# A two-expert weighted sum: the last two tiles in one slot, and twelve product rows in place of ten on GpSimd

## The chip, the core and the metric

The kernel runs on one core of a Trainium2 chip. The core has engines that run side by side and wait for each other through semaphores: VectorE (DVE in the profile), ScalarE (ACT), GpSimd (POOL), TensorE (PE, not used here) and SyncE (SP, which here only issues transfers). Sixteen DMA engines move data between the chip's main memory (HBM) and the core's own memory (SBUF, 128 partitions). The metric is the device time of one execution in microseconds; the median over several runs is compared.

## The reference

For each of 16 x 1,024 = 16,384 tokens there are two expert outputs of 512 float32 values and two weights. The result is their weighted sum:

```
weights = combine_weights[..., np.newaxis]            # (16, 1024, 2, 1)
np.sum(expert_outputs * weights, axis=2)              # (16, 1024, 2, 512) -> (16, 1024, 512)
```

So 67.1 MB are read, 33.6 MB are written, and each output value takes two multiplications and one addition.

## The kernel before, in words

Each partition handles 128 tokens (`per`), in nine tiles (`sizes`): seven of 16 tokens, numbered 0 to 6, and two of 8, numbered 7 and 8. The first 120 tokens of every partition lie together in one region of the input, the last 8 in another (`rows`, line 37). A token is 4 KB in a partition: 1,024 float32, expert 0 and then expert 1. Seen as rows of 512 values, a tile of 16 tokens has 32 product rows.

A loop over the tiles (line 73) writes down for each:

- **A slot.** `et` (line 74) is taken from a pool of three slots, each large enough for 16 tokens. The tile that takes a slot for the fourth time and later has to wait until the store of the tile three places earlier has landed. So the load of tile 3 waits for the store of tile 0, and so on; the load of tile 7 waits for the store of tile 4, the load of tile 8 for the store of tile 5.
- **The load** (line 80), issued by SyncE. Tile 0 is loaded in two pieces.
- **The products**, tiles 0 to 6: GpSimd multiplies the last 10 of the 32 rows in place (line 117, `theirs`), VectorE the first 22 (line 122, `mine`). VectorE takes its weights from a copy in PSUM (`pw`), GpSimd from SBUF (`wt`). GpSimd's product is made to wait for the sum of the previous tile (line 121).
- **The sum** (line 123), on VectorE, of the two halves of each token. The result is packed into the front of the same slot (`ot`, line 76).
- **The store** (line 127), issued by ScalarE for tiles 0 to 6 and by SyncE for tiles 7 and 8.

Tile 7 is split in another way: ScalarE scales expert 0 of five tokens (line 114), GpSimd of three (line 117), and VectorE scales expert 1 (line 122) and adds (line 123). Tile 8 goes token by token: ScalarE scales expert 0 (line 88), and VectorE multiplies expert 1 and adds in one instruction (line 91). Both are the same before and after.

Each engine carries out its own instructions in the order written, and each queue issues its transfers in that order. Loads, and the two last stores, go through SyncE's queue, q1 in the profile; the other stores go through ScalarE's queue, q10. Both are served by the same sixteen DMA engines.

Of the kernel before, what the change touches and what calls it, by code (L numbers as in the profile page):

```python
# [1 line left out]

# [4 lines left out]


@with_exitstack
def kernel(  # L10
    ctx: ExitStack,
    tc: tile.TileContext,
    expert_outputs: bass.AP,
    combine_weights: bass.AP,
    out: bass.AP,
):

    nc = tc.nc
    b, s, k, h = expert_outputs.shape
    assert k == 2
    n = b * s
    P = nc.NUM_PARTITIONS
    per = n // P
    assert per * P == n
    sizes = [16] * 7 + [8, 8]
    J, LAST = max(sizes), sizes[-1]  # L30
    main = per - LAST
    assert sum(sizes) == per
    eo = expert_outputs.rearrange("b s k h -> (b s) (k h)")
    cw = combine_weights.rearrange("b s k -> (b s) k")
    o = out.rearrange("b s h -> (b s) h")

    def rows(x):

        a = x[0 : P * main, :].rearrange("(p t) f -> p t f", p=P)
        b = x[P * main : n, :].rearrange("(p t) f -> p t f", p=P)  # L40
        return lambda t, c: a[:, t : t + c, :] if t < main else b[:, t - main : t - main + c, :]

    eo, cw, o = rows(eo), rows(cw), rows(o)

    dt = mybir.dt.float32
    mult = mybir.AluOpType.mult
    add = mybir.AluOpType.add
    copy = mybir.ActivationFunctionType.Copy

    last = len(sizes) - 1  # L50

    wpool = ctx.enter_context(tc.tile_pool(name="w", bufs=1))
    ipool = ctx.enter_context(tc.tile_pool(name="in", bufs=3))
    ppool = ctx.enter_context(tc.tile_pool(name="pw", bufs=1, space=bass.MemoryType.PSUM))

    wt = wpool.tile([P, per * k], dt)

    for t, c in ((0, main), (main, LAST)):
        nc.scalar.dma_start(  # L59
            out=wt[:, k * t : k * (t + c)].rearrange("p (t k) -> p t k", k=k), in_=cw(t, c)  # L60
        )

    warm = wpool.tile([P, 1], dt)
    nc.scalar.activation(out=warm, in_=nc.const_aps.tensor(1.0, (P, 1), dt), func=copy)  # L64

    pw = ppool.tile([P, per * k], dt)
    nc.vector.tensor_copy(out=pw, in_=wt)  # L67
    w1 = pw.rearrange("p (t k) -> p t k", k=k)
    sync = mybir.DependencyInfo(mybir.DependencyClass.Sync, mybir.DependencyReason.DATA)
    total = None  # L70
    t0 = 0

    for g, c in enumerate(sizes):
        et = ipool.tile([P, J, k * h], dt)

        ot = et.rearrange("p j f -> p (j f)")[:, 0 : J * h].rearrange("p (j f) -> p j f", f=h)
        ek = et.rearrange("p j (k h) -> p (j k) h", k=k)

        for a, m in ((0, 2), (2, c - 2)) if g == 0 else ((0, c),):
            nc.sync.dma_start(  # L80
                out=et[:, a : a + m],
                in_=eo(t0 + a, m),
                max_dma_last_dim=k * h * 4 if g + a == 0 else None,
            )
        if g == last:
            for i in range(c):
                t = t0 + i
                nc.scalar.activation(  # L88
                    out=et[:, i, 0:h], in_=et[:, i, 0:h], func=copy, scale=wt[:, 2 * t : 2 * t + 1]
                )  # L90
                nc.vector.scalar_tensor_tensor(  # L91
                    out=ot[:, i, :],
                    in0=et[:, i, h : 2 * h],
                    scalar=wt[:, 2 * t + 1 : 2 * t + 2],
                    in1=et[:, i, 0:h],
                    op0=mult,
                    op1=add,
                )
        else:
            if g < last - 1:  # L100

                a, b = 2 * (c - 5), 2 * c
                mine, theirs = ek[:, 0:a], ek[:, a:b]
                wv = pw[:, 2 * t0 : 2 * t0 + a].unsqueeze(2)
                wp = wt[:, 2 * t0 + a : 2 * t0 + b].unsqueeze(2)
            else:

                m = c - 3
                mine, theirs = et[:, 0:c, h : 2 * h], et[:, m:c, 0:h]
                wv = w1[:, t0 : t0 + c, 1:2]  # L110
                wp = wt.rearrange("p (t k) -> p t k", k=k)[:, t0 + m : t0 + c, 0:1]
                for i in range(m):
                    t = t0 + i
                    nc.scalar.activation(  # L114
                        out=et[:, i, 0:h], in_=et[:, i, 0:h], func=copy, scale=wt[:, 2 * t : 2 * t + 1]
                    )
            p = nc.gpsimd.tensor_tensor(  # L117
                out=theirs, in0=theirs, in1=wp.to_broadcast(list(theirs.shape)), op=mult
            )
            if total is not None:  # L120
                tc.add_manual_dep(p.ins, total.ins.name, sync, reason="the shared port")
            nc.vector.tensor_tensor(out=mine, in0=mine, in1=wv.to_broadcast(list(mine.shape)), op=mult)  # L122
            total = nc.vector.tensor_tensor(  # L123
                out=ot[:, 0:c], in0=et[:, 0:c, 0:h], in1=et[:, 0:c, h : 2 * h], op=add
            )
        queue = nc.scalar if g < last - 1 else nc.sync
        queue.dma_start(out=o(t0, c), in_=ot[:, 0:c])
        t0 += c

# [1 line left out]
_INS = ['expert_outputs', 'combine_weights']  # L131
_OUTS = [((16, 1024, 512), 'float32')]


# [23 lines left out]
```

## Time and profile before

| | |
|---|---|
| median of 5 runs | 243.13 us (242.01 to 244.05) |
| profiled execution, its own time | 242.97 us |
| its span | 241.2 us |
| VectorE busy | 158.6 us |
| GpSimd busy | 64.0 us |
| ScalarE busy | 9.7 us |
| moved | 100.80 MB, 418 GB/s over the span |
| load of tile 7 issued / tile 8 issued | 183.00 us / 206.02 us |
| stores of tiles 6, 7, 8 issued | 214.66, 223.54, 229.23 us |

The profile is of one execution. All times inside it count from the start of its span; what lies around the span (1.8 us here) is in the execution's time and not in the trace. A group of instructions is shown with its total busy time, the mean duration of one in ns, and the idle time of its engine just before it with what ended that idle time. The row of DMA slices gives the mean busy share of the sixteen DMA engines in tenths.

### The profile page before, as it was taken

The numbers are of one execution on the slowest core, as the hardware profiler recorded it, in microseconds if no ns is written. First come the engines' busy times: TensorE is split into PE (matmuls) and PEld (weight loads), VectorE is DVE, ScalarE is ACT, GpSimd is POOL, SyncE is SP. The second block draws the span as 40 slices with busy tenths as digits, with TensorE's granted clock in tenths as the row PEclk, the third lists the DMA queues.
The fourth block names the chain that finished last, engine by engine and source line by source line (L and its number), as shares of the span: only waits on it lengthen the run. The fifth ranks groups of instructions, "written<-read, shape, count | busy, mean of one in ns | idle before, by whom it ended". The sixth has DMA issues, their size and how long they took to land.

```text
span 241.2 us, 165 instructions
## 1 busy us (share of the span) xinstructions
DVE 158.6 (66%) x25; ACT 9.7 (4%) x15; POOL 64.0 (27%) x12
## 2 busy tenths in 40 slices
DVE  0001999999749990059982999149990089999900
ACT  2000000000000000000000000000000000221600
POOL 0001920670049000058002920049000086030000
DMA  9998989989989989999989899989999899999994
GB/s 347 457 400 383 522 348 522 348 359 429 516 348 435 522 348 435 435 435 435 522 348 495 375 462 467 435 370 435 397 489 435 359 435 435 386 435 402 399 432 185
DMA packets 3152, 100.80 MB, mean 418 GB/s; under 512 B 464, under 2 KB 592, under 8 KB 848
## 3 DMA queue, kind: packets, MB, share of 16 engines
q1 hardware_dynamic: 1856, 71.30, 69.6%
q10 hardware_dynamic: 1296, 29.49, 28.5%
HBM read 67.24 MB, written 33.55 MB: 418 GB/s over the span
## 4 chain that ended last, share of the span: by engine, by line
DMA 55%; DVE 35%; another core or an unknown queue 2%; ACT 2%; issue 1%; ACTq 0%; DVEq 0%; SPq 0%
DMA out_dram<-et 24%; DMA et<-in_expert_outputs_dram 22%; DVE et L122 20%; DVE et L123 14%; DMA wt<-in_combine_weights_dram 9%; ACT et L88 2%; DVE et L91 1%; DVEq L153 0%; ACTq L153 0%; ACTq L59 0%; DVE pw L67 0%; DVEq L123 0%; SPq L80 0%; ACTq L88 0%
## 5 line engine op out<-in xcount | busy, mean ns | idle before, releaser
L122 DVE TENSOR_TENSOR et<-et,pw 128x11264 f32<-128x11264 f32 (+1 forms) x8 | 87.6, 10952 | 46.4 <-DMA et<-in_expert_outputs_dram 46.4
L117 POOL TENSOR_TENSOR et<-et,wt 128x5120 f32<-128x5120 f32 (+1 forms) x8 | 63.8, 7979 | 153.2 <-DMA et<-in_expert_outputs_dram 111.3
L123 DVE TENSOR_TENSOR et<-et 128x8192 f32<-128x8192 f32 (+1 forms) x8 | 65.3, 8158 | 0.9
L67 DVE COPY pw<-wt 128x256 f32<-128x256 f32 x1 | 0.4, 428 | 23.1 <-DMA wt<-in_combine_weights_dram 23.1
L114 ACT ACTIVATE et<-et,wt 128x512 f32<-128x512 f32 x5 | 3.2, 709 | 206.4 <-DMA et<-in_expert_outputs_dram 206.4
L91 DVE SCALAR_TENSOR_TENSOR et<-et,wt 128x512 f32<-128x512 f32 x8 | 5.6, 745 | 0.2
L88 ACT ACTIVATE et<-et,wt 128x512 f32<-128x512 f32 x8 | 5.0, 712 | 9.2 <-DMA et<-in_expert_outputs_dram 9.2
L64 ACT ACT_TABLE_LOAD x1 | 1.3, 1283 | 1.7 <-PEq L142 1.7
L64 ACT ACTIVATE warm<-const-float32-1.0 128x1 f32<-128x1 f32 x1 | 0.2, 203 | 0.0
L142 POOL MEMSET const-float32-0.0<- 128x1 f32 x1 | 0.1, 99 | 0.2 <-issue 0.2
L142 POOL MEMSET const-bfloat16-1.0<- 128x1 bf16 x1 | 0.1, 102 | 0.0
L142 POOL MEMSET const-uint8-127<- 128x1 uint8 x1 | 0.1, 102 | 0.0
L142 POOL MEMSET const-float32-1.0<- 128x1 f32 x1 | 0.1, 99 | 0.0
## 6 DMA issues: line engine op xcount, KB each, us to landing
out_dram<-et ACTq DMA_DIRECT2D x7, 4096.0 KB, 29.0
et<-in_expert_outputs_dram SPq DMA_DIRECT2D x2, 4096.0 KB, 21.3
et<-in_expert_outputs_dram SPq DMA_DIRECT2D x1, 7168.0 KB, 21.7
out_dram<-et SPq DMA_DIRECT2D x2, 2048.0 KB, 11.4
et<-in_expert_outputs_dram SPq DMA_DIRECT2D x1, 1024.0 KB, 5.2
wt<-in_combine_weights_dram ACTq DMA_DIRECT2D x1, 120.0 KB, 4.2
et<-in_expert_outputs_dram SPq DMA_DIRECT2D x6, 37.1
wt<-in_combine_weights_dram ACTq DMA_DIRECT2D x1, 8.0 KB, 21.8
```

The lines of the kernel that those rows point to most:

```text
L64: nc.scalar.activation(out=warm, in_=nc.const_aps.tensor(1.0, (P, 1), dt), func=copy)
L67: nc.vector.tensor_copy(out=pw, in_=wt)
L88: nc.scalar.activation(out=et[:, i, 0:h], in_=et[:, i, 0:h], func=copy, scale=wt[:, 2 * t : 2 * t + 1])
L91: nc.vector.scalar_tensor_tensor(out=ot[:, i, :], in0=et[:, i, h : 2 * h], scalar=wt[:, 2 * t + 1 : 2 * t + 2], in1=et[:, i, 0:h], op0=mul ...
L114: nc.scalar.activation(out=et[:, i, 0:h], in_=et[:, i, 0:h], func=copy, scale=wt[:, 2 * t : 2 * t + 1])
L117: p = nc.gpsimd.tensor_tensor(out=theirs, in0=theirs, in1=wp.to_broadcast(list(theirs.shape)), op=mult)
L122: nc.vector.tensor_tensor(out=mine, in0=mine, in1=wv.to_broadcast(list(mine.shape)), op=mult)
L123: total = nc.vector.tensor_tensor(out=ot[:, 0:c], in0=et[:, 0:c, 0:h], in1=et[:, 0:c, h : 2 * h], op=add)
L142: nc = _bacc.Bacc("TRN2", target_bir_lowering=False, num_devices=1)
```

## The change

Two things change.

1. Tile 8 no longer takes a slot of its own. Tiles 7 and 8, 8 tokens each, share one 16-token slot: tile 7 in its first half, tile 8 in its second. The only wait for that slot is the one at tile 7's load, for the store of tile 4; tile 8's load is next on SyncE's queue and has no wait of its own. The store of tile 5 is no longer waited for before the end.
2. In tiles 0 to 6 GpSimd multiplies 12 of the 32 product rows and VectorE 20. For GpSimd this is 6,144 elements in a partition where it was 5,120, for VectorE 10,240 where it was 11,264.

The number and the order of the instructions on each engine are the same.

```
-        et = ipool.tile([P, J, k * h], dt)
+        both = both[:, J - c : J] if g == last else ipool.tile([P, J, k * h], dt, name="et")
+        et = both[:, 0:c]

-        ot = et.rearrange("p j f -> p (j f)")[:, 0 : J * h].rearrange("p (j f) -> p j f", f=h)
+        ot = et.rearrange("p j f -> p (j f)")[:, 0 : c * h].rearrange("p (j f) -> p j f", f=h)
...
             if g < last - 1:

-                a, b = 2 * (c - 5), 2 * c
+                a, b = 2 * (c - 6), 2 * c
                 mine, theirs = ek[:, 0:a], ek[:, a:b]
```

## The prediction

> **What bounds the kernel now.** I read the page's slices first, because a kernel that moves 100.8 MB and computes little should be measured against its transfers.
>
> ```profile
> span 241.2 us, 165 instructions
> DVE 158.6 (66%) x25; ACT 9.7 (4%) x15; POOL 64.0 (27%) x12
> ...
> DMA  9998989989989989999989899989999899999994
> ...
> HBM read 67.24 MB, written 33.55 MB: 418 GB/s over the span
> ```
>
> The DMA row stands at 8 or 9 in every slice but the last. No compute engine is busy beyond 66%. Next I read stretches of the span (columns: stretch, its length, then busy us and instruction count of VectorE, ScalarE and GpSimd, granted clock, DMA share, GB/s).
>
> ```profile
> 0.00:4.00 4.00, 0.00 (x0) 1.49 (x2) 0.20 (x4) 1.00 0.52 162
> ...
> 84.00:124.00 40.00, 25.34 (x3) 0.00 (x0) 8.73 (x1) 1.00 0.97 419
> 124.00:160.00 36.00, 22.22 (x3) 0.00 (x0) 8.73 (x1) 1.00 1.00 432
> 160.00:183.00 23.00, 20.58 (x2) 0.00 (x0) 8.73 (x1) 1.00 1.00 417
> 183.00:206.00 23.00, 11.95 (x2) 0.00 (x0) 8.72 (x1) 1.00 0.99 426
> 206.00:222.00 16.00, 15.87 (x3) 3.17 (x5) 2.75 (x1) 1.00 1.03 416
> 222.00:232.00 10.00, 6.99 (x9) 5.01 (x8) 0.00 (x0) 1.00 0.95 410
> 232.00:237.40 5.40, 0.00 (x0) 0.00 (x0) 0.00 (x0) 1.00 0.98 422
> 237.40:241.20 3.80, 0.00 (x0) 0.00 (x0) 0.00 (x0) 1.00 0.15 65
> ```
>
> The last column but one is the answer: from 4 us to 237.4 us the 16 DMA engines have work in hand all the time (shares a little over 1 come from putting a packet into the stretch where it starts). They are empty only at the start, and thin in the last 3.8 us. The last packets explain that tail: eleven engines finish between 237.3 and 237.8, five between 239.3 and 239.8. The five fell behind around 163 to 171 us, where some 64 KB reads took 3.0 to 3.5 us and the usual one takes 2.42. At the best steady rate here, 434 GB/s, 100.8 MB take 232.3 us. The other 8.9 us of the span are start (2.6), slow packets and uneven engines, and the closing waits (1.4, from the last packet at 239.8 to 241.2).
>
> The groups by shape and the waits say the same from the compute side.
>
> ```profile
> L122 DVE TENSOR_TENSOR et<-et,pw 128x11264 f32<-128x11264 f32 x7 | 83.2, 11886 | 46.4 <-DMA et<-in_expert_outputs_dram 46.4
> L117 POOL TENSOR_TENSOR et<-et,wt 128x5120 f32<-128x5120 f32 x7 | 61.1, 8726 | 141.2 <-DMA et<-in_expert_outputs_dram 111.3 <-issue 17.4 <-DVE et L123 12.5
> L123 DVE TENSOR_TENSOR et<-et 128x8192 f32<-128x8192 f32 x7 | 60.8, 8692 | 0.7
> ...
> L122 DVE TENSOR_TENSOR et<-et,pw 128x4096 f32<-128x4096 f32 x1 | 4.4, 4414 | 0.0
> ...
> L117 POOL TENSOR_TENSOR et<-et,wt 128x1536 f32<-128x1536 f32 x1 | 2.8, 2750 | 12.0 <-DVE et L123 12.0
> ```
>
> VectorE waits 46.4 us for loads ahead of its product. The chain of waits alone misleads: it gives VectorE 35% of the span, because a load waits for a store and a store for a sum. But while one tile goes round that loop, other transfers fill the DMA engines. A shorter loop only helps if it fills an empty DMA slot, and there is none in the middle.
>
> **What the Trainium skill says.** "DMA: Bandwidth & Descriptors", section "Queues, rings and completion order": each DMA engine goes round the queues with work, a packet at a time, and takes one queue's descriptors in ring order. The trace agrees: between 203 and 205 us every engine alternates one 32 KB read and one 32 KB write, 1.21 us each, and tile 8's reads start only behind tile 7's. The same page, "Where 436 GB/s comes from", puts the ceiling at 435 GB/s; the steady 434 stands on it. "SBUF — State Buffer", "Who interferes with whom": VectorE with two SBUF inputs excludes a GpSimd operation that reads SBUF, with one it does not, and DMA contends with neither. The product reads its weights from PSUM, and indeed 11,264 elements take the same 11.89 us in all seven tiles with GpSimd beside them.
>
> **Part 1, the shared slot.** Before, tile 8's load waits for the store of tile 5, which lands at 205.94; the load is issued at 206.02. After, it stands behind tile 7's load (issued 183.00) with no wait of its own, so it is issued near 183.3, 22.7 us sooner. What it gains is only what the DMA engines were missing. They weren't: tile 7's own reads hold the queue until 207.2 on the fast engines and 209.2 on the late five, so tile 8's reads cannot start sooner than that. On the first eight or nine engines they arrive just in time: their first packets took 1.6 to 2.15 us and not 1.21, about 0.6 us each. Early issue may remove that, but these are engines that have 2 us to spare at the end. Value 0, ends -0.6 and 0. Nothing new queues behind the load on SyncE: the next there is the store of tile 7 at 223.5. Tile 8's data and products stay as they are; VectorE and ScalarE drop a wait that was over long before.
>
> **Part 2, twelve rows.** The slope between the two product sizes is (11.886 - 4.414)/(11264 - 4096) = 1.042 ns an element, so 1,024 fewer elements give 11.886 - 1.067 = 10.82 us. GpSimd: (8.726 - 2.750)/(5120 - 1536) = 1.667 ns, so 8.726 + 1.707 = 10.43 us. GpSimd starts 0.07 to 0.16 us after VectorE, ends at 10.59, and the sum still waits for VectorE, with 0.23 us of margin. So a tile's compute is 1.07 us shorter, in seven tiles 7.5 us of VectorE time. It all lands in the wait for loads. Each of the seven stores is issued about 1.07 us sooner, and moves ahead of reads that then move back; bytes and rate stay. Value 0.
>
> **The tail, where it could cost.** The store of tile 6 is issued at 214.66, while tile 8's load runs alone. Issued 1.07 us sooner (213.6) it takes every second packet from that load sooner, both being 32 KB, so tile 8's load lands up to 1.1 us later than 221.96. The last sums and the last store (229.23) follow: 230.3. That store needs 2.1 MB / 422 GB/s = 5.0 us of DMA, and about 1.2 us from issue to first packet. Today the engines are full until 237.4, so it arrives 237.4 - 229.23 - 5.0 - 1.2 = 2.0 us before the others would run dry. After, 0.9 us are left. Cost 0; beyond another 0.9 us the end moves one for one.
>
> **Sum.** 241.2 + 0 + 0 + 0 = 241.2 us of span, and with the 1.8 us around it that the profiled execution has (242.97 - 241.2) 243.0 us. This execution stands 0.16 us under the median of 243.13. I say 243.0.
>
> **Rivals.**
> - *Better order, faster.* The early load closes the just-in-time gap (0.6), and the shifted stores break up the slow packets that put five engines 2 us behind. Removing both entirely bounds the gain: the tail's work is 0.15 x 3.8 = 0.6 us for all 16, so balanced engines end near 238.0 instead of 239.8, 1.8 us, and with 0.6 about 240.6; half of it gives 241.7. For: the slow packets are 2 to 3 us after a change in the queues. Against: other such changes (72, 94, 184 us) show none.
> - *Last store late, slower.* The tail's cushion of 2.0 us is used up. It takes a last store issued later than 231.2. With tile 8's load landing 3.5 us later (three packets more of the store of tile 6 ahead of it than now) the cost is 1.5 us: 244.5. For: tile 6's store does come sooner, and everything after the last load is serial. Against: that is three times what I work out.
> - *GpSimd becomes the bound of a tile.* If its 6,144 elements take over 10.7 us, the sum waits for it. Even at 13 us a tile would still have slack (4.9 to 14.6 us of wait before most products), and only tiles 0 and 1 follow each other without; stores come later, DMA stays full: about 243.
>
> **How the numbers follow.** I take half a per cent, 1.2 us, as what a measurement of this kernel tells from no change; the five times span 2.0. No change, GpSimd's rival included, 0.57, with 242.0 to 244.0 as its own range; better order 0.24, mostly between 240.9 and 241.8; late last store 0.19, mostly between 244.3 and 245. The range 241.0 to 244.6 leaves out about one in ten at each side.
>
> **What would show it.** Product rows of 10.8 us and GpSimd rows of 10.4; more VectorE wait for loads by some 7 us; tile 8's load issued within half a us of tile 7's, and landing no earlier than 221; a DMA share still at 0.97 or more from 4 us to 237 us. A DMA share clearly under 1 between 225 and 235 us with the last store's issue beyond 231 would say the slower rival; all engines ending within 1 us of each other, near 238, the faster one.

## The result, and the profile after

The changed kernel takes 241.51 us (median of 27 runs, 239.23 to 243.26) against 242.89 us (48 runs of the kernel before, 241.43 to 244.24). The ratio is 0.991, 95% interval 0.989 to 0.993: faster, where I had forecast no change. The ratio of the two medians is 0.994; the 0.991 lies below it because it leaves out, for each kernel, executions over 1.5% above that kernel's fastest, and a quarter of the changed kernel's are such. Nine of its 27 executions lie between 239.2 and 239.8 us; no execution of the kernel before is that short. The profiled execution took 239.31 us and belongs to those nine, so its trace shows 3.7 us of change in the span (241.2 to 237.5) where the medians differ by 1.4.

The page of the changed kernel, the lines that answer to those shown of before:

```profile
span 237.5 us, 163 instructions
...
DVE 151.2 (64%) x25; ACT 9.7 (4%) x15; POOL 76.0 (32%) x12
...
DMA  9979989979989899989898989989989999999996
...
HBM read 67.24 MB, written 33.55 MB: 424 GB/s over the span
```

VectorE lost 7.4 us of work and GpSimd gained 12.0, and the slices look as full as before. The mean rate rose from 418 to 424 GB/s. Its groups by shape (busy us, mean ns of one, idle time ahead):

```profile
L124 DVE TENSOR_TENSOR et<-et,pw 128x10240 f32<-128x10240 f32 x7 | 75.7, 10820 | 49.2 <-DMA et<-in_expert_outputs_dram 49.1
L119 POOL TENSOR_TENSOR et<-et,wt 128x6144 f32<-128x6144 f32 x7 | 73.0, 10433 | 127.3 <-DMA et<-in_expert_outputs_dram 101.5 <-issue 16.1 <-DVE et L125 9.7
L125 DVE TENSOR_TENSOR et<-et 128x8192 f32<-128x8192 f32 x7 | 60.8, 8692 | 0.7
```

The two prices, 10.82 and 10.43 us, are those that I worked out. Now stretches of the span of the changed kernel (stretch, length, busy us and count of VectorE, ScalarE and GpSimd, clock, DMA share, GB/s):

```profile
124.00:160.00 36.00, 20.05 (x3) 0.00 (x0) 10.43 (x1) 1.00 1.01 437
160.00:183.00 23.00, 19.51 (x2) 0.00 (x0) 10.43 (x1) 1.00 1.05 456
183.00:206.00 23.00, 15.63 (x2) 0.00 (x0) 10.43 (x1) 1.00 0.95 410
206.00:222.00 16.00, 13.05 (x4) 4.34 (x7) 2.75 (x1) 1.00 0.99 426
222.00:232.00 10.00, 5.15 (x8) 3.83 (x7) 0.00 (x0) 1.00 0.98 419
```

The last two columns have to be read together. A packet is counted whole in the stretch where it starts, so both columns swing by some per cent, in the same direction; their quotient is the rate while a DMA engine has a packet in hand, and that swings far less. Here it is 433, 434, 432, 430 and 428 GB/s, close to one value throughout. The table that the prediction shows of the kernel before has 432, 417, 430, 404 and 432 in the same five stretches. In two of them, 160 to 183 and 206 to 222 us, the engines were marked busy and moved less. I had read the share alone, saw 1.00 and 1.03, and concluded that nothing was missing. A slow packet is busy time too.

The two slow stretches begin where a load is issued late. In the kernel before, tile 6's load is issued at 159.86, when tile 5's has all but landed (160.08), and tile 8's at 206.02, just ahead of the end of tile 7's reads (207.2 on most engines). The second stretch has slow packets twice. The first packets of tile 8's load, at 207.2, take 1.6 to 2.15 us on eight engines where 1.21 is usual, and 21 more reads of that load, from 216.1 to 218.8 us, take 1.5 to 2.4, just after tile 6's store was issued at 214.66. The prediction counted the first and not the second, which is this line of the kernel before, 367 GB/s at a share of 1.00:

```profile
215.00:220.00 5.00, 4.87 (x2) 0.00 (x0) 2.46 (x1) 1.00 1.00 367
```

SyncE's queue of the changed kernel has both loads sooner:

```profile
156.71 0.33 SPq L82 DMA_DIRECT2D et<-in_expert_outputs_dram  x1
```

```profile
185.71 0.33 SPq L82 DMA_DIRECT2D et<-in_expert_outputs_dram  x1
```

The first is tile 6's load, 3.15 us sooner. The second is tile 7's, with tile 8's directly behind it at 186.08. After 50 us no packet of the changed kernel is slow (no 64 KB one takes over 2.5 us, no 32 KB one over 1.25), and the sixteen DMA engines end within 0.5 us of each other (235.7 to 236.1), where five used to end 2 us behind.

So two late loads are gone. The experiments ask which part of the change removed which, what each is worth, and whether being late is what costs.

### The profile page after: what moved, and what is told of

Its sections match the earlier page's. It is cut to its first block, busy times and chain, and to the rows that moved or that the text cites. A ratio compares the mean times of both kernels' runs of the same rounds, so it can differ in the third digit from the quotient of the medians.

```text
span 237.5 us, 163 instructions
## 1 busy us (share of the span) xinstructions
DVE 151.2 (64%) x25; ACT 9.7 (4%) x15; POOL 76.0 (32%) x12
## 4 chain that ended last, share of the span: by engine, by line
DMA 67%; DVE 25%; ACT 2%; ACTq 0%; DVEq 0%; issue 0%; SPq 0%
DMA et<-in_expert_outputs_dram 30%; DMA out_dram<-et 28%; DVE et L124 14%; DVE et L125 11%; DMA wt<-in_combine_weights_dram 9%; ACT et L90 2%; DVE et L93 1%; DVEq L155 0%; ACTq L155 0%; ACTq L59 0%; DVE pw L67 0%; SPq L82 0%; DVEq L125 0%; DVEq L67 0%
## 5 line engine op out<-in xcount | busy, mean ns | idle before, releaser
L119 POOL TENSOR_TENSOR et<-et,wt 128x6144 f32<-128x6144 f32 (+1 forms) x8 | 75.8, 9472 | 136.5 <-DMA et<-in_expert_outputs_dram 101.5
L124 DVE TENSOR_TENSOR et<-et,pw 128x10240 f32<-128x10240 f32 (+1 forms) x8 | 80.2, 10019 | 49.2 <-DMA et<-in_expert_outputs_dram 49.1
```

Source lines behind the costliest of these rows:

```text
L119: p = nc.gpsimd.tensor_tensor(out=theirs, in0=theirs, in1=wp.to_broadcast(list(theirs.shape)), op=mult)
```

## The experiments

### One part at a time

*The slot alone* keeps ten rows on GpSimd in the changed kernel:

```
-                a, b = 2 * (c - 6), 2 * c
+                a, b = 2 * (c - 5), 2 * c
```

> The shared slot alone, with GpSimd still at 10 rows. Slot theory (tile 8's load behind tile 7's means no engine waits for work after the store of tile 5, and no engine's lateness is passed on through that wait): the whole gain, ratio 0.991, about 241.5 us, lowest runs near 239.3. Rows theory (stores that come 1.07 us sooner end together on all engines, so that tile 6's load is issued near 156.7 and not 159.9): no gain, ratio 1.000, and tile 6's load issued near 159.9. Slow-packet theory (neither edit matters, the loss is drawn afresh each time): anything between.

*The rows alone* keep a slot for each tile, in the kernel before:

```
-                a, b = 2 * (c - 5), 2 * c
+                a, b = 2 * (c - 6), 2 * c
```

> Twelve rows on GpSimd alone, each tile with its own slot. Slot theory: ratio 1.000, about 242.9 us, no run under 241.4. Rows theory: the whole gain, ratio 0.991, tile 6's load issued near 156.7, all engines ending within 0.5 us of each other. If both are needed: between, or no gain in either run.

Measured: the slot alone 241.46 us, ratio 0.993 (0.990 to 0.996). The rows alone 242.73 us, ratio 0.999 (0.996 to 1.001). By the medians the slot does it. The single executions say more: three of the slot alone's 13 took 239.15 to 239.38 us, as short as the changed kernel's best, and five of the rows alone's 22 took 245.7 to 246.3, longer than any of the kernel before beside them (244.86 at most). No profile shows what happened in those five. The changed kernel again, on the same chip:

> The changed kernel again, beside the others: 0.991 of before, single executions from 239.3 to 243.3. If its profile is of an execution at 241 us or more, the slow-packet theory expects slow packets after the issue of a store or load, as before the change, and the rows theory expects tile 6's load near 156.7 in it nevertheless.

It gave 239.43 us in six executions, ratio 0.988 (0.983 to 0.992); its profile is again of a short execution (239.37), so it can't say what a long one looks like. Each of the single parts removes one of the late loads and keeps the other. Two shorter stretches, 162 to 172 and 206 to 217 us, of the kernel before:

```profile
162.00:172.00 10.00, 10.00 (x1) 0.00 (x0) 6.96 (x1) 1.00 1.01 400
206.00:217.00 11.00, 11.00 (x2) 3.17 (x5) 2.29 (x1) 1.00 1.07 429
```

of the changed kernel:

```profile
162.00:172.00 10.00, 9.90 (x2) 0.00 (x0) 8.98 (x1) 1.00 1.06 459
206.00:217.00 11.00, 10.87 (x3) 3.17 (x5) 2.75 (x1) 1.00 0.99 429
```

of the rows alone:

```profile
162.00:172.00 10.00, 9.90 (x2) 0.00 (x0) 9.14 (x1) 1.00 1.06 459
206.00:217.00 11.00, 10.87 (x3) 3.17 (x5) 2.75 (x1) 1.00 0.92 334
```

and of the slot alone:

```profile
162.00:172.00 10.00, 10.00 (x1) 0.00 (x0) 7.19 (x1) 1.00 1.00 380
206.00:217.00 11.00, 11.00 (x2) 3.17 (x5) 2.75 (x1) 1.00 1.01 435
```

Rate over share: 433 and 363 GB/s with the rows alone, 380 and 431 with the slot alone, 396 and 401 before, 433 and 433 after. The rows mend the first stretch, the slot the second. This is why the rows alone bring nothing: tile 6's load comes in time (156.77), all sixteen engines stay together, and then all sixteen run out at 207. Tile 7's reads end at 206.8 to 207.1, and tile 8's load is issued only here:

```profile
206.32 0.33 SPq L80 DMA_DIRECT2D et<-in_expert_outputs_dram  x1
```

Its first packets start at 207.3 and later, and take up to 2.1 us. Up to 206 us this trace agrees with the changed kernel's second one to within 0.2 us in every issue and in the time at which each load and store has landed. After it the span is 240.1 against 237.6. The wait for the store of tile 5 costs 2.5 us there. Of these the engines stand empty for 0.5 us; another 1.65 us for each engine is what 48 reads between 207.3 and 215.0 us take over the usual 1.21, most of those after 210 between the issue of tile 6's store (209.11) and its first writes (213.6 and later). What the rows gained at 163 was given back at 207.

### The step of the rows the other way

GpSimd takes eight rows, in the kernel before:

```
-                a, b = 2 * (c - 5), 2 * c
+                a, b = 2 * (c - 4), 2 * c
```

> Eight rows on GpSimd, 24 on VectorE, own slots: the step of the rows the other way, each store 1.07 us later. Rows theory: slower than before, by up to as much as twelve rows gain, about 244 us (1.005), with tile 6's load at 160 or later. Slot theory: 1.000. If what counts is where a store meets the round of packets and not how early it is, this may as well be faster.

Measured 247.32 us, ratio 1.020 (1.016 to 1.025), more than any theory said, and for another reason. The instructions of an engine need not stand in the order of the loop: in the kernel before, too, ScalarE runs tile 7's scalings (209.65) ahead of tile 6's store (214.66). With the longer product on VectorE the scheduler puts tile 7's product ahead of tile 6's sum. VectorE's instructions of that kernel, and the store that waits for them:

```profile
210.20 4.42 DVE L122 TENSOR_TENSOR et<-et,pw 128x4096 f32<-128x4096 f32 x1 [3.92 <-DMA et<-in_expert_outputs_dram]
214.54 8.69 DVE L123 TENSOR_TENSOR et<-et 128x8192 f32<-128x8192 f32 x1
223.26 0.34 ACTq L127 DMA_DIRECT2D out_dram<-et  x1
```

VectorE stands idle for 3.92 us until tile 7's load has landed, does tile 7's product, and only then tile 6's sum, which ends at 223.23. So tile 6's store is issued at 223.26 instead of 214.66. (Two scalings of tile 8 stand ahead of that store on ScalarE as well, but they end before the sum.) By then nothing is left to transfer:

```profile
219.00:223.50 4.50, 4.50 (x2) 1.34 (x2) 0.20 (x1) 1.00 0.02 7
```

4.5 us without DMA, and 4.5 us of time lost (247.32 against 242.84 beside it). So this run says little on the rows. It says what a truly empty DMA costs here: about its own length.

### How late is too late for tile 8's load

If only the running out matters, tile 8's load can be held back a good while without loss, and loses sharply after that. In the changed kernel it is made to wait for GpSimd's product of tile 6:

```
+            if g == last:
+                tc.add_manual_dep(ld.ins, p6.ins.name, sync, reason="a later load")
```

> The changed kernel, with tile 8's load held back until GpSimd's product of tile 6 is done, near 200.7 us: 14 us later than in the changed kernel, 6 us ahead of the end of tile 7's reads (207.2). Gap theory (the load only has to be in its queue before the queue runs out): no loss against the changed kernel, ratio about 0.990, no slow packets at 207. Slot theory in its wider form (the load must stand behind tile 7's from the start): as with rows alone, 0.998.

or for VectorE's sum of tile 6:

```
-                tc.add_manual_dep(ld.ins, p6.ins.name, sync, reason="a later load")
+                tc.add_manual_dep(ld.ins, s6.ins.name, sync, reason="a later load")
```

> The changed kernel, with tile 8's load held back until VectorE's sum of tile 6 is done, near 209 us: 2 us after tile 7's reads have ended, and some 3 us later than with slots of their own. Gap theory: the queues stand empty from about 207 to 210 us, the loss is 3 us of empty DMA and the slow packets after it: 243.5 to 246 us, ratio 1.003 to 1.012. If lateness were absorbed elsewhere: about 0.998 as with rows alone.

The first was issued at 200.89 in its profile:

```profile
200.89 0.33 SPq L82 DMA_DIRECT2D et<-in_expert_outputs_dram  x1
```

and lost nothing: 239.28 us in four executions, ratio 0.987 (0.983 to 0.991), span 237.5, the stretch 206 to 217 at 429 GB/s with a share of 0.99. Fifteen microseconds later is free as long as six are left.

The second came out worse than expected: 251.48 us, ratio 1.033 (1.028 to 1.038). In its profile tile 8's load is issued at 213.69, since in that execution tile 6 itself was late, and the DMA engines stand empty:

```profile
208.50:214.50 6.00, 6.00 (x2) 3.17 (x5) 0.76 (x1) 1.00 0.00 0
```

Then tile 8's load and tile 6's store start together and share the engines, so the load lands at 236.26 and the last store is issued at 242.85, with the transfers running out a second time before it (a share of 0.19 from 240 to 244 us). My 3 us of empty DMA were too few: I counted one gap, and the delay of the last load makes a second.

Together with the rows alone this is a curve, for tile 8's load with twelve rows: issued at 186 or 201 us, spans of 237.5; at 206.3, 240.1; at 213.7, 250.2, of which about 1.2 us belong to slow packets at 164 to 170 us, after a late load of tile 6. The second run also answers a rival, that the place of tile 8 in memory and not the time of its load makes its packets slow: here the slot is shared, and 15 of the load's reads, from 214.7 us on, take 1.75 to 2.7 us.

### Why tile 6's load is late or not

Tile 6's load waits for the store of tile 3. That store is 8 packets on each engine, and each takes its turn with a 64 KB read, 2.42 + 1.21 = 3.6 us a round. So I supposed that 1.07 us decide whether a last packet gets into one round or falls into the next. The test changes the rows of tile 3 only, in the changed kernel: twelve there and ten elsewhere,

```
-                a, b = 2 * (c - 6), 2 * c
+                a, b = 2 * (c - (6 if g == 3 else 5)), 2 * c
```

> Shared slot, twelve rows on GpSimd in tile 3 alone, ten in the others. Landing-round theory (the 1.07 us of tile 3's store decide whether tile 6's load is issued near 156.7 or near 159.5, and so whether its queue runs out): tile 6's load near 156.7, no slow packets at 163 to 171, profile as of the changed kernel (span 237.5), more executions near 239.3 than with the slot alone. If all rows count: as the slot alone, 0.993, slow packets at 163.

or ten there and twelve elsewhere:

```
-                a, b = 2 * (c - 6), 2 * c
+                a, b = 2 * (c - (5 if g == 3 else 6)), 2 * c
```

> Shared slot, ten rows in tile 3 alone, twelve in the others. Landing-round theory: tile 6's load near 159.5, slow packets at 163 to 171, time as the slot alone, about 241.5 us, ratio 0.993. If the other tiles' rows carry it: tile 6's load near 156.7 and executions near 239.3 in the majority.

Measured: twelve in tile 3 alone 239.89 us, ratio 0.988 (0.985 to 0.992); ten in tile 3 alone 241.55 us, ratio 0.993 (0.991 to 0.996). The first is as the changed kernel at its best (0.988), the second as the slot alone; the two intervals just meet. Their stretch from 162 to 172 us, first with twelve and then with ten in tile 3:

```profile
162.00:172.00 10.00, 10.00 (x1) 0.00 (x0) 8.16 (x1) 1.00 1.05 455
```

```profile
162.00:172.00 10.00, 9.71 (x1) 0.00 (x0) 9.64 (x1) 1.00 1.05 400
```

The same share and 55 GB/s apart. Of the first, two expectations failed. Its tile 6 load came at 158.72 and not 156.7, because the store of tile 3 (issued at 125.17) landed at 156.4 on most engines and at 158.64 on one. It was still in time. That one engine is 1.1 us behind at the end too, and the span is 238.5 and not 237.5. The profile with ten rows in tile 3 is of a long execution (243.39 us) in which one engine is behind from tile 2's load on: tile 3's load landed at 106.61 on it, so tile 3's store is 2.8 us later than in the changed kernel, of which the rows explain 1.07. For the rows of tile 3 the median of its 22 executions is the evidence, and the profile only for what a late store does.

One row for each of several profiles, from the timelines of ScalarE's and SyncE's queues, and rate over share from 162 to 172 us:

| kernel | store of tile 3 issued | load of tile 6 issued | GB/s while busy |
|---|---|---|---|
| tile 3 on three engines (below) | 122.42 | 154.33 | 432 |
| tile 8's load at 201 | 124.46 | 156.69 | 435 |
| changed kernel | 124.58 | 156.71 | 433 |
| rows alone | 124.62 | 156.77 | 433 |
| twelve in tile 3 | 125.17 | 158.72 | 433 |
| before | 125.67 | 159.86 | 396 |
| tile 8's load at 214 | 126.03 | 159.93 | 382 |
| slot alone | 126.08 | 159.30 | 380 |
| ten in tile 3 | 127.35 | 159.49 | 381 |
| eight rows | 127.60 | 160.57 | 379 |

There is a clean step between 125.2 and 125.7 us, and it follows tile 3's store, not the number of rows: the kernel with tile 8's load at 214 has twelve rows everywhere, and was late in that execution because tile 3's own load landed at 106.36 on its last engine, where 104.9 is usual. The four profiles that the table leaves out (two more of the changed kernel and two of the next section) have tile 3's store at 123.9 to 124.6, tile 6's load at 156.65 to 157.01 and no slow packet at 163.

The landings of tile 3's store go in steps, as supposed, of 2.3 to 3.4 us. Issued at 122.42, it landed at 153.8 to 154.3 on all engines; at 124.58, at 156.2 to 156.6; at 125.67, at 156.2 to 156.4 on eleven and at 159.7 on five; at 126.08, at 156.6 on three and at 158.8 to 159.2 on thirteen. Tile 6's load waits for the last engine.

### A version with more room

If tile 3's store is what matters, it can be given more room. ScalarE, idle until tile 7, takes 8 of its rows, and VectorE 16 and GpSimd 8:

```
-                a, b = 2 * (c - 6), 2 * c
-                mine, theirs = ek[:, 0:a], ek[:, a:b]
+                z, a, b = (8, 24, 32) if g == 3 else (0, 20, 32)
+                mine, theirs = ek[:, z:a], ek[:, a:b]
...
+                for r in range(z):
+                    nc.scalar.activation(
+                        out=ek[:, r], in_=ek[:, r], func=copy, scale=wt[:, 2 * t0 + r : 2 * t0 + r + 1]
+                    )
```

> The changed kernel, with tile 3's products spread over three engines: ScalarE 8 rows (8 x 0.62 us = 5.0), VectorE 16 (8.7 us), GpSimd 8 (7.0 us). Tile 3's store then comes 2.1 us sooner still, near 122.5, and has 2.7 us more before it misses its round. Landing-round theory: tile 6's load at 156.7 or sooner, no slow packets at 163, and most single executions near 239.3: median 239.3 to 240, ratio 0.985 to 0.989. If the executions of 241 to 243 us that the changed kernel shows have another cause: median 241.5 and 0.991 as there.

and with the condition `g < 6`, so that tiles 0 to 5 do the same:

> The same split over three engines in tiles 0 to 5. Each of their stores comes 2.1 us sooner, tile 1's and 2's by more. Landing-round theory: as with tile 3 alone, ratio 0.985 to 0.989, since nothing but tile 3's store decides; below 239.0 us no execution, since the transfers bound it. If earlier stores help in themselves: below 0.985. If another store now falls into a bad round: slow packets elsewhere, 0.99 to 1.00.

Tile 3 alone: 239.71 us, ratio 0.988 (0.985 to 0.991), five of six executions under 240 us. Tiles 0 to 5: 241.07 us, 0.992 (0.989 to 0.995). Earlier stores do not help in themselves. In that kernel tile 6's load comes in time too (157.01), and 433 GB/s while busy follow, but ten 64 KB reads at 77.4 us are slow (2.9 to 3.0 us), where the other profiles have none to six. They are worth 0.3 us for each engine, and the profile is of a short execution (240.10), so they do not explain the median. The one with tile 3 alone was run again beside the changed kernel:

> Tile 3's products over three engines, again, beside the changed kernel on one chip: ratio to the kernel before 0.988, most single executions between 239.2 and 240. Landing-round theory: fewer executions over 241 us than in the changed kernel. Other cause of those: as many.

> The changed kernel beside it: ratio 0.988 to 0.992, a third of the executions near 239.3, others from 241 to 243.3. If both kernels have the same spread of executions here, tile 3's earlier store bought nothing over the changed kernel.

Medians of 239.94 and 241.74 us; ratios 0.985 (0.981 to 0.989) and 0.986 (0.981 to 0.991), the second from three of six executions, since the other three took over 243 us. Of twelve executions in both runs together two took over 241 us; of the changed kernel's 39, twenty did. That points to tile 3's store for a part of the changed kernel's long executions, but the intervals overlap, and one of the twelve took 243.44. The profile of the second run shows another part: its execution took 240.94 us with both loads in time and no slow packet after 78 us. There 21 reads from 44.0 to 48.5 us, as the first store's writes begin, took up to 3.75 us, and five engines are 1 to 2 us behind from tile 2's load (71.7 against 69.7 us) to the end. This version is faster than the kernel before; that it is faster than the changed kernel is likely and not shown.

## Why the prediction was wrong

**The bound was right.** The range of 241.0 to 244.6 us even holds the 241.51, but in the part that was the faster rival's; the case that I put first, no change, was wrong. DMA bounds every version: no execution in all these runs lies under 239.1 us, and where DMA stood empty (eight rows, tile 8's load at 214) the time was lost at once.

**Part 1, the shared slot: the step that failed.** I gave it "Value 0, ends -0.6 and 0", since tile 8's reads follow tile 7's anyway and arrive "just in time" on engines "that have 2 us to spare". The order was right, the load issued 0.37 us behind tile 7's as forecast. The price of just in time was not. The profile before showed eight engines lose 0.6 us each at 207; with all sixteen together, as in the rows alone, all run out, their first packets are slow, and the reads are slow again around the start of tile 6's store, at 210 to 215 us. That second group stood in the profile before, too (216 to 219 us, 0.7 us for each engine), and had no term in the sum. The mis-sized term is 2.5 us in the profiles (240.1 against 237.6) and 1.4 us in the medians (slot alone against before).

**Part 2, twelve rows.** The prices were right to 0.01 us. "bytes and rate stay. Value 0" is right for this part alone in the medians (0.999), and wrong as to why. The 1.07 us of one store, tile 3's, moved a load by 3.15 us and the rate of one stretch from 396 to 433 GB/s. That only shows in the time when tile 8's load is in time as well: the slot with twelve rows in tile 3 gives 0.986 to 0.991 in five runs, with ten 0.993 in two, and the intervals touch. The count of short executions is clearer: of at most 240.3 us there are 16 in 39 of the changed kernel, and 5 in 35 of the two kernels with the slot and ten rows in tile 3. So the rows change how often a short execution comes, and the medians of the slot alone and of the changed kernel are the same. In the profiles the slot alone has a span of 239.1 and the changed kernel 237.5.

**The reading behind both.** "there is none in the middle" was drawn from the DMA share. My own table had the two stretches in its last column, 417 and 416 GB/s, and I explained the missing microseconds as "slow packets and uneven engines", as if they were a property of the chip. In the profile before, five engines fell behind after the first late load. Late loads are not the only way to that: in the second run with tile 3 on three engines five are behind from 71 us on, with every later load in time. Two smaller statements were off as well. One read and one write by turns stand in the trace up to 203.2 us, and from there to 205 only reads. VectorE's wait for loads rose by 2.7 us (46.4 to 49.1) and not by some 7, because the whole span became shorter.

**The tail.** Tile 8's load landed at 220.80, 1.2 us sooner than before and not up to 1.1 us later; the last store was issued at 227.38 and not at 230.3. The argument of shared packets held on the eleven engines that were ahead: on them the load landed at 218.2 to 218.6 before and at 220.3 to 220.8 after, with tile 6's store issued 4.75 us sooner (209.91) and not 1.07. But ScalarE waits for the last engine, and the five that landed at 221.5 to 221.96 are now level with the others. The slower rival had no room, and it appeared only where it was forced (tile 8's load at 214, where the last load landed 14 us late).

**The faster rival** had the gap at tile 8's load and the vanishing of the slow packets, and its 240.6 to 241.7 holds the median, though its single executions reach from 239.2 to 243.3. Its second half was a shot in the dark: "the shifted stores break up the slow packets" names no store. It is tile 3's, by whether the next load comes in time. Against it I counted that other changes in the queues show no slow packets; that is true and not enough.

**What stays open.** Why packets are slow after a late load, when the other queue has work, is not shown. A queue that ran out is not enough either: tile 3's load, issued at 72 us with its queue empty since 69.7, is followed by none in the kernel before (by one to ten, at 77 us, in six of the fourteen profiles). All profiles have at least sixteen slow packets when the first store's writes begin (at 46 us, in three of them from 44 us on), 0.7 to 1.4 us that none of these edits removes. And a quarter of the changed kernel's executions take 243 us, of which no profile was taken. The one profile of so long an execution with the shared slot, ten rows in tile 3 (243.39), shows a single DMA engine falling behind: tile 2's load landed at 72.13 on it and at 69.73 or sooner on the others, tile 8's at 226.05 and 221.34, and the last store was issued at 232.63 instead of 227.38. Whether the changed kernel's long executions are like that is not shown.

## What to carry to other kernels

In a kernel bound by transfers, divide the rate by the DMA share in each stretch, and look for stretches in which the engines are busy and slow. Then look at what was issued just before: a load that arrives when its queue is running out can cost more than the gap that it leaves (here 2.5 us for a gap of 0.5), and six microseconds of lead were enough. When a small edit moves one transfer past a round of packets, its effect can be a step and not a slope, and two such edits have to be judged together, since each can hand its gain to the other's bottleneck. Compare single executions as well as medians: a step shows in how many of them are short.

## What the runs showed of the hardware

- A load that was issued 0.5 to 0.8 us ahead of the end of the reads before it in its queue (206.32 against 206.8 to 207.1) had its first packets at 207.3 and later, and cost 2.5 us of span; one issued 6 us ahead (200.89) cost nothing.
- A store beside 64 KB reads lands in steps: issued at 125.67, the store of tile 3 landed at 156.2 to 156.4 us on eleven engines and at 159.7 on five; issued 1.1 us sooner, at 156.6 or sooner on all sixteen.
- Slow packets count as busy. From 162 to 172 us two kernels had the same DMA share, 1.05, and moved 455 and 400 GB/s.
